# S5 discretisation on VectorE, projection tiles behind every scan batch, and four merge gates kept in HBM

## The chip, the cores and the metric

The kernel runs on one core of a Trainium2 chip, as one program, launched once. The metric is device time in microseconds. A core has five engines that run on their own and wait for each other by semaphores: TensorE (PE, matrix products into PSUM), VectorE (DVE), ScalarE (ACT), GpSimd (POOL) and SyncE (SP). DMAs are issued from queues of SP, ACT and POOL. Everything here is in float32, or in float32 pairs: a value is split into a rounded part `hi` and a rest `lo`, and a product is three matmuls (hi x hi, lo x hi, hi x lo).

## The reference

One step of a diffusion backbone of two layers on 512 latent tokens and 128 context tokens (T = 640 columns, D = 1024). Each layer computes, with two conditioning vectors (one per kind of token):

```python
shift, scale, gate = split(silu(cond) @ w_mod + b_mod)
h = rms_norm(x) * (1 + scale) + shift
u_a, g_a, u_b, g_b, u_c, g_c, m = split(h @ w_in)
y_a = GLU(gelu(S5_bidirectional(u_a))) * silu(g_a)     # 32 groups, 64 complex states each
y_b = Hyena2(short_conv(u_b)) * silu(g_b)              # two implicit long convolutions
y_c = pooling(u_c) * silu(g_c)
x = x + gate * (sum over b of sigmoid(m_b) * (y_b @ w_br_b)) @ w_out
```

The S5 recurrence is x[t] = a x[t-1] + B u[t] with complex a per state. Its coefficients come from the parameters by a discretisation: `dt = exp(log_dt)`, `a = exp(lam * dt)`, `k = (a - 1) / lam`, `B = k * b`. Beside the outputs y for both kinds of tokens the final S5 states of the context are returned.

## The kernel before, in words

**Projection tiles.** `h` lies in SBUF as `hhi` and `hlo`, eight blocks of 128 features by 640 tokens. `w_in` has 56 tiles of 128 output features. `win` (which calls `linear`) makes one tile: two weight chunks of 128x512 are loaded by SP (`wr`, three buffers), ACT casts each to `wh` (L238), DVE makes the rest `wl` (L239), and PE runs 4 x 3 matmuls of 320 columns for each chunk and each half of the tokens (L261 to L263), 48 in all. A callback evicts each half from PSUM, for which there are three buffers.

**Stages.** The *head* loads x, squares it, makes the modulation vectors (`mod_chunk`, L404, 2 MB of weights each, and `mod_turn`, L415), the filter network (`mlp`), the S5 discretisation for both layers (`s5_disc`, `exp_`, `s5_disc2`, `s5_bb`) and `h` (`make_h`), and puts the Hyena filters of layer 0 into HBM (`filter`). Then each layer runs:
- `layer`: `u_a` (four projection tiles, through HBM into another order), then eight scan batches (`s5_gen` makes matrices and rotations for four groups, with `kd` stored to HBM by SP and scattered back by eight DMAs into `mt`, L914; `s5_run` makes the inputs `pz`, the scans `kk` on DVE, L961 and L962, the output `yp`, L974 and L976, and the GELU, stored to `yd`). After the eight batches, in the program's text, twelve `conv_u` tiles (short convolution, evicted into `raw`, L996) and four `gate_b` tiles (SiLU into `sgb`, L1012; POOL multiplies).
- `glu` (four SiLU gates `sga`, then the GLU), the Hyena convolutions, the pooling branch, and the first merges.
- `merges`: for branch a one tile at a time (`merge`), for b and c two tiles at a time (`merge2`, eight calls per layer). `merge2` takes the two gate tiles of the projection from `win2` (L333 to L335), which forms them with seven products of 12 matmuls in place of eight by adding up blocks of weights and of `h` beforehand (`win2_prep`, on DVE), and then multiplies them onto the branch's product (`branch`, L1225, 24 matmuls for each tile). In layer 0 a modulation chunk for later use goes between the calls.
- `out_proj` and the norm.

**What sets the order.** Nothing is ordered by hand. The instructions are put into each engine's queue by a planner at compile time. The order of the program's text is its priority; it simulates the engines and takes an instruction of lower priority when those before it are not ready. Once planned, the queues are fixed: on the chip an engine waits for the next instruction of its queue, whatever else is ready, and the same holds for SP's and POOL's DMA queues.

The discretisation works on tiles of 128x64 (two directions of 64 states, and for both layers 32 groups), its powers on up to 128x256, and `s5_bb` on 128x512. It is a chain of some hundred instructions on POOL, with three activations on ACT (two sines and an absolute value, L746 to L748) and a reciprocal on DVE.

Of the kernel before, what the change touches and what calls it, by code (L numbers as in the profile page):

```python
# [14 lines left out]
ALU = mybir.AluOpType  # L15
# [207 lines left out]
class Body:  # L223
    def __init__(self, nc, tc, I, O, dbg=None):
        self.nc, self.tc, self.I, self.O, self.dbg = nc, tc, I, O, dbg or {}
        self.smod, self.sacc = {}, {}
# [473 lines left out]
    def exp_(self, pool, x):  # L700
        nc = self.nc
        v = nc.gpsimd
# [11 lines left out]
        v.tensor_scalar(o, c, 1.0 / 40320, 1.0 / 5040, op0=ALU.mult, op1=ALU.add)  # L714
        for f in (720, 120, 24, 6, 2, 1, 1):
            v.tensor_tensor(out=o, in0=o, in1=c, op=ALU.mult)
            v.tensor_scalar(o, o, 1.0 / f, None, op0=ALU.add)
        v.tensor_scalar(q, q, 127.0, 8388608.0, op0=ALU.add, op1=ALU.mult)
        v.tensor_copy(qi, q)
        v.tensor_tensor(out=o, in0=o, in1=qi.bitcast(F32), op=ALU.mult)  # L720
        return o

    def s5_disc(self, Q, S):
        nc, I = self.nc, self.I
        v = nc.gpsimd
        w = DEPTH * G
        sp = Q.tile([P, 5, DEPTH, G], F32, name="sp")
        for l in range(DEPTH):
            nc.sync.dma_start(sp[:, :, l], I['s5p'][l])
# [61 lines left out]
    def s5_bb(self, Q, S, l, kre, kim):  # L791
# [5 lines left out]
        self.cmul(nc.gpsimd, Q, self.bb[:, 0], self.bb[:, 1], kb(kre), kb(kim), sm[:, 0], sm[:, 1], [G, H], "cb")  # L797

    def s5_disc2(self, Q, S, pw, rs):
        nc = self.nc  # L800
        nc.gpsimd.dma_start(self.pwd, pw[:, :, :, 1])
        nc.gpsimd.dma_start(self.rsd, rs[:, :, 1])
# [204 lines left out]

    def silu_tile(self, l, nt, dst):
        nc = self.nc

# [197 lines left out]
    def merge2(self, l, n, br, ys):  # L1208
        ths = [self.M.tile([P, 644], F32, tag="t", name="mth", bufs=4)[:, 0:T] for _ in range(2)]
        self.win2(l, 32 + 8 * br + n, ths)  # L1210
# [64 lines left out]
    def run(self):  # L1275
        tc, nc = self.tc, self.nc
        with tc.tile_pool(name="dram", bufs=1, space=DRAM) as self.DR, \
# [10 lines left out]
            self.setup()  # L1288
# [7 lines left out]
            with self.pool("mod0") as M, self.pool("filt0") as F:  # L1296
                with self.pool("disc", side="left") as Q, self.pool("mlp", side="left") as FM:
                    fh = self.mlp(FM, fh)
                    wins = F.tile([P, 5, 512], F32, name="wins")
                    fr = F.tile([P, 3, 2, 3 * P], F32R, name="fr")  # L1300
                    self.setup_par()
                    self.mod_open(0, M)
                    self.load_x0(X, 0)
                    for kk in range(KD):
                        self.square(X, kk, 0)
# [10 lines left out]
                    self.s5_disc2(Q, SP, *dd)  # L1316
# [170 lines left out]
```

## Time and profile before

| | |
|---|---|
| median of 3 runs (lowest to highest) | 1569.88 us (1569.44 to 1576.25) |
| the profiled execution: own time, span | 1571.28 us, 1569.3 us |
| mean granted TensorE clock of it | 0.957 of full speed |
| PE busy | 1447.5 us, 92% of the span, 10764 matmuls |
| DVE busy | 1144.9 us, 73% |
| ACT busy | 683.2 us, 44% |
| POOL busy | 624.7 us, 40% |
| DMA | 173.49 MB, mean 111 GB/s |

The profile is of one execution. Busy times are sums of what the engine's instructions cover; issuing a DMA and waiting are not counted. The granted clock is the share of TensorE's full speed that the chip allowed; its two levels are 1.2 and 2.4 GHz. A bracket behind a row of a timeline says how long the engine stood before it and what it waited for. The shares over the whole span hide that the stages have different limits, so the rows below go by stages.

### The profile page before, as it was taken

Reading aid. Unit: us, or ns where it says so; the run is one execution under the profiler, and the core shown is the slowest. Engines: PE = TensorE matmul, PEld = TensorE weight load, DVE = VectorE, ACT = ScalarE, POOL = GpSimd, SP = SyncE. Lnnn points to the kernel's source line nnn. Section 1 sums busy time; section 2 is a strip of 40 time slices with the busy share of each in tenths; the row PEclk is TensorE's granted clock in tenths of the full one; section 3 lists DMA queues with packets and bytes.
Section 4 is the critical chain, followed back from the end, with each engine's and each line's share of the span. In section 5 each row is a group of like instructions: output and inputs, shape, how many; then the busy total and the mean of one; then the engine's idle time right before and its main releaser. Section 6 shows DMA issues by size and latency. Waiting matters only on the chain.

```text
span 1569.3 us, 28424 instructions
## 1 busy us (share of the span) xinstructions
PE 1447.5 (92%) x10764; PEld 1381.5 (88%) x10764; DVE 1144.9 (73%) x1896; ACT 683.2 (44%) x1474; POOL 624.7 (40%) x608
## 2 busy tenths in 40 slices
PE   4769898899999999999998788879999999999997
PEld 2458897899999998999997788879999999999996
DVE  6688899945777795555577888996377779766665
ACT  3166454525333443444334655453443334444443
POOL 5917254320344325454323635542015243566411
PEclk8789989999999999999999988989999999999998
DMA  9424312243222334554652342122532213222154
GB/s 311 158 72 118 98 53 70 69 122 107 91 75 81 102 121 135 184 172 137 190 181 100 104 114 60 52 69 84 146 96 83 74 61 121 82 83 85 36 168 155
DMA packets 114944, 173.49 MB, mean 111 GB/s; under 512 B 30360, under 2 KB 54568, under 8 KB 114297
## 3 DMA queue, kind: packets, MB, share of 16 engines
q1 hardware_dynamic: 113433, 165.33, 34.4%
q0 software_dynamic: 1296, 6.19, 1.2%
q8 instruction: 85, 1.39, 0.4%
q14 instruction: 50, 0.41, 0.1%
q10 hardware_dynamic: 80, 0.16, 0.0%
HBM read 150.08 MB, written 21.56 MB: 109 GB/s over the span
## 4 chain that ended last, share of the span: by engine, by line
PE 64%; DVE 16%; issue 6%; DMA 5%; POOL 3%; ACT 3%; SPq 2%; POOLq 0%; DVEq 0%; ACTq 0%
PE mm L261 13%; PE mm L262 13%; PE mm L263 13%; PE mm L333 4%; PE mm L335 4%; PE mm L334 4%; DVE wl L239 2%; PE modp L404 2%; PE inva L1131 1%; PE invb L1131 1%; DVE kk L962 1%; DVE kk L961 1%; DVE i L874 1%; DMA wr<-w_in 1%; DMA yr<-yd 1%
## 5 line engine op out<-in xcount | busy, mean ns | idle before, releaser
L261 PE MATMUL mm<-hhi,wh 128*128 128x320 f32 x1280 | 404.9, 317 | 21.9 <-ACT raw L996 12.3
L263 PE MATMUL mm<-hhi,wl 128*128 128x320 f32 x1280 | 400.1, 315 | 7.4 <-DVE wl L239 7.4
L262 PE MATMUL mm<-hlo,wh 128*128 128x320 f32 x1280 | 403.3, 315 | 2.5 <-DVE hlo L665 1.8
L239 DVE TENSOR_TENSOR wl<-wr,wh 128x512 fp32r<-128x512 f32 x312 | 258.8, 831 | 106.2 <-ACT wh L238 98.6
L238 ACT CAST wh<-wr 128x512 fp32r<-128x512 f32 x312 | 192.7, 618 | 247.2 <-PE mm L262 172.1
L261 PEld LDWEIGHTS mm<-hhi,wh 128*128 128x128 f32 x1280 | 246.2, 192 | 27.0 <-ACT raw L996 13.7
L263 PEld LDWEIGHTS mm<-hhi,wl 128*128 128x128 f32 x1280 | 245.3, 192 | 8.2 <-DVE wl L239 7.9
L262 PEld LDWEIGHTS mm<-hlo,wh 128*128 128x128 f32 x1280 | 246.1, 192 | 4.6 <-DVE hlo L665 2.2
L875 POOL TENSOR_TENSOR i<-i,i 128x1024 f32<-128x1024 f32 x16 | 45.2, 2822 | 136.7 <-DVE i L873 104.1
L262 PE MATMUL mm<-mlo,wh 128*128 128x320 f32 x256 | 79.6, 312 | 0.5 <-DVE mlo L242 0.4
L261 PE MATMUL mm<-mhi,wh 128*128 128x320 f32 x256 | 79.0, 312 | 0.9 <-DVE X L1249 0.6
L333 PE MATMUL mm<-hhi,wh 128*128 128x320 f32 x256 | 79.8, 312 | 0.0
L335 PE MATMUL mm<-hhi,wl 128*128 128x320 f32 x256 | 79.4, 310 | 0.0
L263 PE MATMUL mm<-mhi,wl 128*128 128x320 f32 x256 | 78.8, 309 | 0.4 <-DVE wl L239 0.4
L334 PE MATMUL mm<-hlo,wh 128*128 128x320 f32 x256 | 79.0, 309 | 0.0
L239 DVE TENSOR_TENSOR wl<-ws,wh 128x512 fp32r<-128x512 f32 x64 | 54.4, 849 | 31.4 <-ACT wh L238 30.1
L1225 DVE SCALAR_TENSOR_TENSOR mth<-mth,mm 128x320 f32<-128x320 f32 x64 | 31.2, 488 | 54.8 <-PE mm L263 54.8
L238 ACT CAST wh<-ws 128x512 fp32r<-128x512 f32 x64 | 39.7, 620 | 71.9 <-PE mm L334 36.3
L339 DVE TENSOR_TENSOR mth<-mm,mth 128x320 f32<-128x320 f32 x80 | 39.2, 491 | 34.7 <-PE mm L335 18.1
L335 PE MATMUL mm<-thi,wl 128*128 128x320 f32 x192 | 60.6, 316 | 0.0
L333 PE MATMUL mm<-thi,wh 128*128 128x320 f32 x192 | 60.5, 315 | 0.0
L873 POOL TENSOR_TENSOR ow<-cw,po 128x512 f32<-128x512 f32 x32 | 45.9, 1451 | 34.7 <-PE yp L976 34.6
(424 smaller groups left out, 3988.5 us busy)
## 6 DMA issues: line engine op xcount, KB each, us to landing
wr<-w_in SPq DMA_DIRECT2D x224, 256.0 KB
wm<-w_mod SPq DMA_DIRECT2D x48, 512.0 KB
wr<-w_out SPq DMA_DIRECT2D x48, 256.0 KB
hd<-hs SPq DMA_DIRECT2D x32, 256.0 KB
hsr<-hd SPq DMA_DIRECT2D x32, 256.0 KB
mt<-kd SPq DMA_DIRECT2D x128, 32.0 KB
wr<-w_br_a SPq DMA_DIRECT2D x16, 256.0 KB
wr<-w_br_b SPq DMA_DIRECT2D x16, 256.0 KB
```

The costliest lines, as they stand in the source:

```text
L238: nc.scalar.copy(hi, src)
L239: nc.vector.tensor_tensor(out=lo, in0=src, in1=hi.bitcast(F32), op=ALU.subtract)
L261: nc.tensor.matmul(ps[i], wh[:, ks], at(hi, k, sl), start=(k == 0), stop=False)
L262: nc.tensor.matmul(ps[i], wh[:, ks], at(lo, k, sl), start=False, stop=False)
L263: nc.tensor.matmul(ps[i], wl[:, ks], at(hi, k, sl), start=False, stop=(k == kt - 1))
L333: nc.tensor.matmul(out, wh[:, ks], xh, start=(k == 0), stop=False)
L334: nc.tensor.matmul(out, wh[:, ks], xl, start=False, stop=False)
L335: nc.tensor.matmul(out, wl[:, ks], xh, start=False, stop=(k == 3))
L339: e.tensor_tensor(out=o, in0=x, in1=y, op=ALU.add)
L404: nc.tensor.matmul(ps[r0:r0 + 32, :], self.cs[:, 2 * hf + q, :], w[:, q, :], start=(hf < 2), stop=(hf >= 2))
L873: eng.tensor_tensor(out=out[:, r], in0=hb(r), in1=pb(0), op=ALU.mult)
L875: e.tensor_tensor(out=out, in0=out, in1=tmp, op=ALU.add)
```

## The change

Five parts:
1. The discretisation (`exp_`, `s5_disc`) runs on DVE in place of POOL, with multiply and add fused into one instruction (the Horner steps of `exp_` are seven `scalar_tensor_tensor`). Its parameters `s5p` are loaded by `s5_load`, which is called before `setup`, so these are the first loads of the kernel.
2. `s5_bb` of layer 0 runs on DVE (that of layer 1 stays on POOL), and the two stores of `s5_disc2` (`pwd`, `rsd`, the values for layer 1) are issued from ACT's queue in place of POOL's.
3. In the head `s5_disc` comes before the squares, and `filter_load` and `s5_disc2` earlier among the modulation turns.
4. The twelve `conv_u` and four `gate_b` tiles, and four new ones, are called behind the scan batches, three and two in turn (3, 2, 3, 2, 3, 2, 3, 2), in place of after all eight.
5. The four new ones are the gate tiles 40 to 43 of the projection, the first four of branch b: `ahead` makes each with `win` (48 matmuls), evicts it with the tanh and stores it in HBM (`gd`, 128x640). `merge2` loads such tiles in place of calling `win2`, so two of the eight `merge2` of each layer have no `win2`. (`silu_tile` has the same test; no tile that it makes is kept.)

```diff
     def exp_(self, pool, x):
-        nc = self.nc
-        v = nc.gpsimd
+        v = self.nc.vector
...
-        v.tensor_scalar(o, c, 1.0 / 40320, 1.0 / 5040, op0=ALU.mult, op1=ALU.add)
-        for f in (720, 120, 24, 6, 2, 1, 1):
-            v.tensor_tensor(out=o, in0=o, in1=c, op=ALU.mult)
-            v.tensor_scalar(o, o, 1.0 / f, None, op0=ALU.add)
-        v.tensor_scalar(q, q, 127.0, 8388608.0, op0=ALU.add, op1=ALU.mult)
-        v.tensor_copy(qi, q)
-        v.tensor_tensor(out=o, in0=o, in1=qi.bitcast(F32), op=ALU.mult)
+        v.tensor_scalar(o, c, 1.0 / 40320, None, op0=ALU.mult)
+        for f in (5040, 720, 120, 24, 6, 2, 1):
+            v.scalar_tensor_tensor(out=o, in0=o, scalar=1.0 / f, in1=c, op0=ALU.add, op1=ALU.mult)
+        v.tensor_scalar(qi, q, 127.0, 8388608.0, op0=ALU.add, op1=ALU.mult)
+        v.scalar_tensor_tensor(out=o, in0=o, scalar=1.0, in1=qi.bitcast(F32), op0=ALU.add, op1=ALU.mult)
         return o
 
+    def s5_load(self, Q):
+        self.sp = Q.tile([P, 5, DEPTH, G], F32, name="sp")
+        for l in range(DEPTH):
+            self.nc.sync.dma_start(self.sp[:, :, l], self.I['s5p'][l])
+
     def s5_disc(self, Q, S):
-        nc, I = self.nc, self.I
-        v = nc.gpsimd
+        nc = self.nc
+        v = nc.vector
...
-        self.cmul(nc.gpsimd, Q, self.bb[:, 0], self.bb[:, 1], kb(kre), kb(kim), sm[:, 0], sm[:, 1], [G, H], "cb")
+        self.cmul(nc.gpsimd if l else nc.vector, Q, self.bb[:, 0], self.bb[:, 1], kb(kre), kb(kim), sm[:, 0], sm[:, 1], [G, H], "cb")
 
     def s5_disc2(self, Q, S, pw, rs):
         nc = self.nc
-        nc.gpsimd.dma_start(self.pwd, pw[:, :, :, 1])
-        nc.gpsimd.dma_start(self.rsd, rs[:, :, 1])
+        nc.scalar.dma_start(self.pwd, pw[:, :, :, 1])
+        nc.scalar.dma_start(self.rsd, rs[:, :, 1])
...
+    def ahead(self, l, nt, func, scale, U):
+        nc = self.nc
+        st = U.tile([P, L642 + 2], F32, tag="raw", name="gst", bufs=2)[:, 0:T]
+
+        def cb(half, ps):
+            nc.scalar.activation(st[:, half * HT:half * HT + HT], ps, func, scale=scale)
+
+        self.win(l, nt, cb)
+        self.gd[l, nt] = self.DR.tile([P, T], F32, name=f"gd{l}_{nt}")
+        nc.sync.dma_start(self.gd[l, nt], st)
...
     def merge2(self, l, n, br, ys):
         ths = [self.M.tile([P, 644], F32, tag="t", name="mth", bufs=4)[:, 0:T] for _ in range(2)]
-        self.win2(l, 32 + 8 * br + n, ths)
+        nt = 32 + 8 * br + n
+        if (l, nt) in self.gd:
+            for i in range(2):
+                self.nc.sync.dma_start(ths[i], self.gd[l, nt + i])
+        else:
+            self.win2(l, nt, ths)
...
-            self.setup()
...
                 with self.pool("disc", side="left") as Q, self.pool("mlp", side="left") as FM:
+                    self.s5_load(Q)
+                    self.setup()
                     fh = self.mlp(FM, fh)
-                    wins = F.tile([P, 5, 512], F32, name="wins")
-                    fr = F.tile([P, 3, 2, 3 * P], F32R, name="fr")
                     self.setup_par()
                     self.mod_open(0, M)
                     self.load_x0(X, 0)
+                    dd = self.s5_disc(Q, SP)
                     for kk in range(KD):
                         self.square(X, kk, 0)
...
-                    dd = self.s5_disc(Q, SP)
+                    wins = F.tile([P, 5, 512], F32, name="wins")
+                    fr = F.tile([P, 3, 2, 3 * P], F32R, name="fr")
+                    self.filter_load(0, F, wins, fr, fh)
                     self.mod_turn(0, 2, self.mod_chunk(0, 2, M, "mm"), "mm")
                     self.mod_turn(0, 3, self.mod_chunk(0, 3, M, "mm"), "mm")
-                    self.filter_load(0, F, wins, fr, fh)
+                    self.s5_disc2(Q, SP, *dd)
                     self.mod_turn(0, 0, self.mod_chunk(0, 0, M, "mm"), "mm")
                     rr = [r for r, _ in self.rinv((0, 1), nc.vector, "mm")]
                     self.mod_turn(0, 1, self.mod_chunk(0, 1, M, "mm"), "mm")
-                    self.s5_disc2(Q, SP, *dd)
...
+            beside = [lambda i=i: self.conv_u(l, i, vx[i // 4][:, i % 4, :], SP) for i in range(12)]
+            beside += [lambda i=i: self.gate_b(l, i, S, vx[2]) for i in range(4)]
+            beside += [lambda i=i: self.ahead(l, 40 + i, AF.Tanh, 0.5, SP) for i in range(4)]
             for b in range(NB):
                 g = self.s5_gen(l, b, S)
                 self.s5_run(l, b, S, g)
+                for _ in range(3 - b % 2):
+                    beside.pop(0)()
             nc.sync.dma_start(self.O['ns'][l], self.nst)
-            for i in range(12):
-                self.conv_u(l, i, vx[i // 4][:, i % 4, :], SP)
-            for i in range(4):
-                self.gate_b(l, i, S, vx[2])
```

## Rows read from the trace of the kernel before

**Rows 1.** Busy time by stage: us, busy (xcount) of each engine, clock, DMA.

```profile
core 0: us, PE busy (x) PEld busy (x) DVE busy (x) ACT busy (x) POOL busy (x), PEclk, DMA share, GB/s
0.00:62.00 62.00, 35.11 (x126) 18.17 (x128) 40.00 (x91) 18.64 (x38) 40.33 (x76) 0.81 0.82 268
62.00:84.00 22.00, 10.68 (x75) 7.99 (x74) 15.99 (x2) 2.85 (x6) 21.52 (x41) 0.68 0.35 101
...
150.00:345.00 195.00, 174.60 (x1642) 169.84 (x1631) 164.91 (x230) 90.52 (x231) 72.58 (x43) 0.93 0.28 77
...
909.00:1104.00 195.00, 174.30 (x1653) 168.34 (x1653) 164.49 (x232) 92.30 (x235) 76.13 (x44) 0.93 0.28 77
...
1341.00:1497.00 156.00, 155.55 (x1060) 154.76 (x1058) 101.50 (x153) 69.15 (x129) 88.62 (x74) 1.00 0.24 72
```

**Rows 2.** Timeline of POOL in the head, first and last of some hundred instructions.

```profile
19.21 3.00 POOL L708 TENSOR_SCALAR ex<-sp 128x64 f32<-128x64 f32 x1 [16.66 <-DMA sp<-s5p]
...
82.30 1.37 POOL L698 TENSOR_TENSOR bb<-cb,cb 128x512 f32<-128x512 f32 x1
```

**Rows 3.** Timeline of ACT in the head.

```profile
46.14 0.26 ACT L746 ACTIVATE q<-q 128x64 f32<-128x64 f32 x1 [9.33 <-POOL q L438]
...
66.62 0.35 ACT L825 COPY rsl<-rs 128x192 f32<-128x192 f32 x1 [9.06 <-POOL rs L779]
```

**Rows 4.** Timeline of DVE in the head, rows for prices by size.

```profile
86.85 0.42 DVE L239 TENSOR_TENSOR flp<-hq,fhp 128x256 fp32r<-128x256 f32 x1
...
88.14 0.16 DVE L606 TENSOR_TENSOR rt<-rt,rx 64x10 f32<-64x10 f32 x1
...
94.22 0.69 DVE L239 TENSOR_TENSOR flo<-hc,fhi 128x512 fp32r<-128x512 f32 x1 [3.02 <-ACT fhi L238]
```

**Rows 5.** Timeline of DVE in the head, around its two long instructions.

```profile
47.25 0.50 DVE L239 TENSOR_TENSOR flp<-hq,fhp 128x256 fp32r<-128x256 f32 x1 [6.24 <-ACT fhp L238]
...
68.01 7.45 DVE L239 TENSOR_TENSOR flo<-hc,fhi 128x512 fp32r<-128x512 f32 x1 [6.69 <-ACT fhi L238]
75.39 8.84 DVE L559 SCALAR_TENSOR_TENSOR hc<-hx,hc 128x512 f32<-128x512 f32 x1
84.15 0.41 DVE L521 TENSOR_TENSOR hq<-fwp,wins 128x256 f32<-128x256 f32 x1
```

**Rows 6.** Evictions on ACT by line, 100 to 420: count, min/median/max ns, first and last start.

```profile
L996 ACT COPY raw<-mm x36: 262/314/431, 155.7 to 307.1; 128x320 f32<-128x320 f32 x12, 128x192 f32<-128x192 f32 x12, 128x128 f32<-128x128 f32 x12
...
L1012 ACT ACTIVATE sgb<-mm x8: 431/436/440, 318.2 to 344.2; 128x320 f32<-128x320 f32 x8
```

**Rows 7.** Timeline of PE, 91 projection matmuls in a row.

```profile
150.71 0.31 PE L261 MATMUL mm<-hhi,wh 128*128 128x320 f32 x1
...
163.91 0.31 PE L261 MATMUL mm<-hhi,wh 128*128 128x320 f32 x1
```

**Rows 8.** PE's groups, 150 to 345: busy us, mean ns | idle before, releaser.

```profile
L261 PE MATMUL mm<-hhi,wh 128*128 128x320 f32 x260 | 83.3, 320 | 6.3 <-ACT raw L996 6.3
...
L976 PE MATMUL yp<-w,ow 128*128 128x81 f32 x128 | 21.4, 294 | 1.3 <-DVE w L968 1.3
L974 PE MATMUL yp<-ug,mt 128*128 128x81 f32 x64 | 13.3, 292 | 9.0 <-DMA wr<-w_in 6.2 <-DMA mt<-kd 2.8
...
L884 PE MATMUL trp<-cst,i 128*128 128x128 f32 x56 | 9.7, 327 | 3.5 <-ACT it L885 3.5
```

**Rows 9.** Chain of waits in layer 0's merges: start, us; two chunks one call apart.

```profile
648.72 1.85 PE modp L404 x16
...
671.03 1.85 PE modp L404 x16
```

**Rows 10.** Busy time of two more stretches, columns as in rows 1.

```profile
583.00:627.00 44.00, 44.00 (x283) 38.29 (x285) 25.19 (x42) 17.13 (x33) 22.98 (x19) 1.00 0.51 166
0.00:40.00 40.00, 18.24 (x50) 9.73 (x50) 26.02 (x68) 14.28 (x28) 20.33 (x39) 0.86 0.95 313
```

**Rows 11.** Timelines of SP's queue and of PE around 285 us.

```profile
282.39 3.60 SPq L914 DMA_DIRECT2D mt<-kd  x8
...
288.43 0.69 PE L974 MATMUL yp<-ug,mt 128*128 128x81 f32 x2 [4.25 <-DMA wr<-w_in]
```

More of the change, by code (lines that the diff above doesn't have):

```diff
@@ L225, in __init__ @@
         self.nc, self.tc, self.I, self.O, self.dbg = nc, tc, I, O, dbg or {}
-        self.smod, self.sacc = {}, {}
+        self.smod, self.sacc, self.gd = {}, {}, {}
     def dump(self, name, ap):
@@ L713, in exp_ @@
         self.madd(v, c, q, hi - math.log(2.0), c, o)
-        v.tensor_scalar(o, c, 1.0 / 40320, 1.0 / 5040, op0=ALU.mult, op1=ALU.add)
-        for f in (720, 120, 24, 6, 2, 1, 1):
-            v.tensor_tensor(out=o, in0=o, in1=c, op=ALU.mult)
-            v.tensor_scalar(o, o, 1.0 / f, None, op0=ALU.add)
-        v.tensor_scalar(q, q, 127.0, 8388608.0, op0=ALU.add, op1=ALU.mult)
-        v.tensor_copy(qi, q)
-        v.tensor_tensor(out=o, in0=o, in1=qi.bitcast(F32), op=ALU.mult)
-        return o
+        v.tensor_scalar(o, c, 1.0 / 40320, None, op0=ALU.mult)
[3 more added lines that the diff above has]
+        v.scalar_tensor_tensor(out=o, in0=o, scalar=1.0, in1=qi.bitcast(F32), op0=ALU.add, op1=ALU.mult)
+        return o
+    def s5_load(self, Q):
+        self.sp = Q.tile([P, 5, DEPTH, G], F32, name="sp")
+        for l in range(DEPTH):
+            self.nc.sync.dma_start(self.sp[:, :, l], self.I['s5p'][l])
     def s5_disc(self, Q, S):
-        nc, I = self.nc, self.I
-        v = nc.gpsimd
+        nc = self.nc
+        v = nc.vector
         w = DEPTH * G
-        sp = Q.tile([P, 5, DEPTH, G], F32, name="sp")
-        for l in range(DEPTH):
-            nc.sync.dma_start(sp[:, :, l], I['s5p'][l])
+        sp = self.sp
         lr, li, ld = sp[:, 0], sp[:, 1], sp[:, 2]
@@ L1006, in conv_u @@
                                        op0=ALU.mult, op1=ALU.add)
+    def ahead(self, l, nt, func, scale, U):
[6 more added lines that the diff above has]
+        nc.sync.dma_start(self.gd[l, nt], st)
     def silu_tile(self, l, nt, dst):
         nc = self.nc
+        if (l, nt) in self.gd:
+            nc.sync.dma_start(dst[:, 0:T], self.gd[l, nt])
+            return
         def cb(half, ps):
@@ L1209, in merge2 @@
         ths = [self.M.tile([P, 644], F32, tag="t", name="mth", bufs=4)[:, 0:T] for _ in range(2)]
-        self.win2(l, 32 + 8 * br + n, ths)
+        nt = 32 + 8 * br + n
+        if (l, nt) in self.gd:
+            for i in range(2):
+                self.nc.sync.dma_start(ths[i], self.gd[l, nt + i])
+        else:
+            self.win2(l, nt, ths)
         for i in range(2):
```

## The prediction

> **What bounds the kernel now.** I read the table of busy time by stage first [rows 1]. TensorE (PE) is the engine that the end hangs on: from the merges of layer 1 on (1341 to 1497 us) it is busy 155.55 of 156 us at a granted clock of 1.00, so whatever PE work is taken out there is taken off the time. Three stretches are different. In the head PE is busy 35.1 of the first 62 us and 10.7 of the next 22, and in the two scan stages (150 to 345 and 909 to 1104, 195 us each) it is busy 174.6 and 174.3 us at a mean clock of 0.93. Those are the places with something to win, and the change works on all three.
>
> **Head.** GpSimd (POOL) carries the S5 discretisation. The timeline of POOL shows it begin at 19.21, when the parameters have landed after an idle 16.66 us, and run almost without a gap to 82.30 + 1.37 = 83.7 us [rows 2]. Three things are seen to wait for it. ScalarE (ACT) stands 9.33 us before the first sine and 9.06 us before the copy of `rsl` [rows 3], and what is queued behind these on ACT makes VectorE (DVE) stand 6.24 and 6.69 us. Then two DVE instructions of 128x512, which cost 0.69 elsewhere [rows 4], take 7.45 and 8.84 us, one after the other, and the second ends when POOL's run ends [rows 5]. That is 6.24 + 6.69 + (7.45 - 0.69) + (8.84 - 0.69) = 27.8 us of DVE. Behind it sit the evictions that PE needs to go on (PE has 10.68 busy us in the 22 from 62 to 84 [rows 1]) and the normalisation of x, which releases the first projection.
>
> What of this goes, and what comes: `exp_` falls from 25 instructions to 15 (its multiply and add pairs are fused) and stands there twice. With range reduction, coefficients and powers DVE gets 81 instructions: 68 of 128x64, one copy and six products of 128x128, six of 128x256; `s5_bb` adds six of 128x512. By the rows of 64x10 at 0.16, 128x256 at 0.42 and 128x512 at 0.69 [rows 4], a straight line gives some 0.2 for 64 and 0.28 for 128 elements: 68 x 0.2 + 7 x 0.28 + 6 x 0.42 + 6 x 0.69 = 13.6 + 2.0 + 2.5 + 4.1 = 22 us. DVE has 62 - 40 = 22 idle us before 62 us [rows 1]; 6.2 of them are the wait just counted, so 16 can take new work, and with its loads first in SyncE's (SP) queue the discretisation can start well before 19 us. I take half of that, 8 us, as used, because the chain is dependent and goes through ACT for the sines. Then 14 us of the 22 lie on DVE's path, and the head ends 27.8 - 14 = **14 us** earlier; bounds 6 (nothing hidden) and 22 (all 16 hidden). The two stores of `pwd` and `rsd` go from POOL's queue to ACT's, at about a microsecond of issue, beside work; nothing. The two loads of `s5p`, now ahead of `cst` and of the loads of the filter network, put these off by about a microsecond, in a time when DVE waits for data anyway; `filter_load`, now ahead of the first modulation turns, moves loads and no work that PE waits for; nothing for both.
>
> Here a rule speaks against the gain. The rows show two DVE instructions held through a row of POOL instructions, which last up to 1.4 us each, for 14.9 us together [rows 2, 5]. The Trainium skill, "SBUF — State Buffer", section "Who interferes with whom", says that a VectorE instruction with two SBUF inputs and a GpSimd instruction that reads SBUF exclude each other, and that the later one waits until the first *instruction* is through. By the letter of it the two waits would be one POOL instruction each, about 2 us, and most of the 14.9 would have some other cause that may stay; by the trace, all of it ends with POOL's run. I go by the trace, and price the other case below.
>
> **Scan stage, each layer.** Before, the twelve `conv_u` tiles already run inside the scan although they are written after it: their evictions run from 155.7 to 307.1, and the four `gate_b` tiles follow as a block, 318.2 to 344.2 [rows 6]. So the order is a planner's, and the new place in the program is a priority, not a command. What is new work is `ahead`: four tiles of 48 matmuls. From 150.71 to 163.91 PE issues 90 of them, 0.147 us each [rows 7]; one tile is 7.05 us, four are **28.2 us** more PE work in the stage. What can take them: PE's waits, 6.3 for evicted tiles, 1.3 and 9.0 before the output products, 3.5 before the transposes, 20 us in all [rows 8], and the clock, 7% of 174.6, 12 us at most. DVE is the engine that could refuse: busy 164.9 of 195 [rows 1]. The tiles add eight weight splits of 0.69, 5.5 us, so some 170 of it would be used; it becomes the second bound, not the first. Most of the waits come from DVE and ACT being late while the convolution tiles press on DVE, and from weights that sit behind the scatter of `mt` in SP's queue. With more filler PE should become the limit, and these engines run ahead of it. I take 12 of the 20 us and 8 of the 12 as used: the stage gets 195 + 28.2 - 12 - 8 = **203 us, 8 longer**. Bounds: nothing used, 28.2 longer; all used, 4 shorter. The four stores of 320 KB per layer are one issue each on SP; each waits for its second eviction, and behind it in SP's queue stand the next weights and the next `mt`. I take nothing, since three weight buffers cover 7 us; if that cover is gone, see the second rival. ACT gets eight evictions and eight casts, some 8 us, and has 104 idle us [rows 1].
>
> **Merges, each layer.** The first two of eight `merge2` lose their `win2`: 7 products of 12 matmuls, 84 x 0.147 = 12.3 us each. The pitch confirms the count: between two modulation chunks lie 671.03 - 648.72 = 22.31 us [rows 9], which is 132 x 0.147 + 1.85 and about a microsecond of `modt`. PE has no gap there, so **24.7 us** go per layer. The `win2_prep` work on DVE stays and has less time before the first `win2` that is left; the two removed ones give DVE about as much back. In layer 0 the modulation chunks come too: two pairs now need 2 x (0.5 + 0.65 + 2.1) = 6.5 MB (weights, kept gates, chunk) in about 20 us, 325 GB/s, against 166 now and 313 in the first 40 us, when the queues were 95% busy [rows 10]. I charge **2 us**, with bounds 0 and 10. Layer 1 has no chunks and pays nothing.
>
> **Sum.** 14 + 2 x (24.7 - 8) - 2 = 45 us off the profiled execution's own 1571.28: 1526. The median of the runs shown, 1569.88, is 1.4 below that execution, so the forecast for a median is 1571.28 - 45.4 - 1.4 = **1524 us**.
>
> **Rivals.** (1) The planner does not do what the program order says, or DVE holds PE back as before, and the 28.2 us lengthen the stage in full: each layer loses 28.2 - 24.7 = 3.5, and only the head gains: 1571.3 - 14 + 7 + 2 - 1.4 = 1565. For it: DVE is busy in 85% of the stage, and more than that while convolution tiles run, since the `gate_b` tiles at its end ask little of it. Against: 30 us of DVE are idle [rows 1], five times what the new splits need. Chance 0.11. (2) **Slower: SP's queue.** In every batch SP issues eight scatters of `mt`, 3.60 us, once `kd` is back from HBM, and the weights stand behind them; at 288.43 PE waited 4.25 us for weights in this way [rows 11]. With five weight loads per batch in place of three, and a store among them, such a wait could fall on each batch: 8 x 4.25 x 2 = 68 us, 1592. It decides from (45 + 8) / 16 = 3.3 us per batch. Against: only 6.2 us of the 9.0 in the row were waits for weights in the whole stage [rows 8]. Chance 0.07. (3) The head does not gain, because DVE, now with 22 us more, ends it as late as POOL did, or because the hold had another cause than POOL's run, which stays: 1524 + 14 = 1538. Chance 0.11. (The rule of the page named above would speak for the second.) (4) PE's waits and clock are all filled: 2 x 12 us more, 1500, and 1494 with some more of the head. Chance 0.11. My forecast has 0.6.
>
> **Numbers.** The range is 1494 to 1558: it holds the forecast, rivals 3 and 4 and the unhidden ends of single terms, and leaves out the slower rival and most of rival 1. About 0.5%, 8 us, is what a measurement of this kernel can tell from no change, so faster means below 1562. Forecast, rivals 3 and 4 and a little of rival 1 make 0.84 faster; the rest of rival 1 makes 0.09 the same; 0.07 slower.
>
> **What would show it.** Right: no DVE instruction of some 8 us before 90 us, and the first projection's evictions some 14 us earlier; `sgb` and the new evictions inside the scan, a stage near 203 us with a clock above 0.93 and fewer PE waits; two merge iterations of about 10 us of PE in each layer with no wait for `mth` or `wm`. Wrong: `ahead` tiles in a block after the last scan; PE waits for `wr<-w_in` in most batches; DVE without a gap to the old end of the head; PE waiting for `wm` in layer 0's merges.

## The result and the profile after

The changed kernel takes **1534.03 us** (median of 4 runs, 1530.10 to 1534.17) against 1572.48 (1569.44 to 1576.25) for the kernel before, run beside it: a ratio of 0.9748 with an interval of 0.9718 to 0.9779, 38 us faster. The forecast was 1524, the range 1494 to 1558; it was set from the 1569.88 known then, and as a gain it is 45.4 us, of which 38.4 came. The profiled execution took 1534.17 us, its span is 1532.4, against 1569.3 before.

First the page of the changed kernel, its parts 1 and 2 (40 slices of 38.3 us):

```profile
span 1532.4 us, 28365 instructions
...
PE 1435.3 (94%) x10812; PEld 1372.2 (90%) x10812; DVE 1125.5 (73%) x1951; ACT 672.0 (44%) x1454; POOL 524.9 (34%) x473
...
PE   3998899999999999999998897989999999999997
...
PEclk9899999999999999999998899999999999999998
```

PE's lower digits are left in the head, in the first part of both scan stages and at the turn between the layers. Now the stretches of [rows 1], moved to where these stages lie now: head (two), scan stage of layer 0, two windows of layer 0's merges with the modulation chunks (against [rows 10]), scan stage of layer 1, merges of layer 1.

```profile
core 0: us, PE busy (x) PEld busy (x) DVE busy (x) ACT busy (x) POOL busy (x), PEclk, DMA share, GB/s
0.00:62.00 62.00, 34.17 (x168) 17.93 (x169) 52.81 (x176) 27.07 (x57) 1.47 (x6) 0.90 0.91 299
62.00:84.00 22.00, 21.22 (x131) 17.18 (x131) 20.91 (x51) 11.93 (x24) 2.39 (x2) 0.89 0.19 73
130.00:343.00 213.00, 196.35 (x1795) 191.04 (x1794) 172.32 (x237) 98.23 (x249) 74.07 (x49) 0.96 0.32 89
560.00:600.00 40.00, 40.00 (x257) 34.01 (x256) 28.23 (x59) 12.54 (x26) 9.51 (x9) 1.00 0.62 204
600.00:640.00 40.00, 40.00 (x276) 37.33 (x275) 20.23 (x34) 16.23 (x31) 18.76 (x16) 1.00 0.54 178
878.00:1092.00 214.00, 196.42 (x1856) 191.45 (x1854) 174.70 (x241) 100.67 (x255) 77.29 (x51) 0.97 0.32 90
1340.00:1460.00 120.00, 119.58 (x815) 118.98 (x813) 75.91 (x113) 53.44 (x99) 67.88 (x57) 1.00 0.23 67
```

Where the time went is read from the starts of a few landmark instructions. The evictions of the changed kernel by line on ACT: `u_a` (L678, the end of the head), `gst` (L1013, the kept gates, now the last thing in the scan stage) and `sgb`, `sga` (both L1026).

```profile
L678 ACT COPY ua<-mm x12: 427/498/752, 88.5 to 129.6; 128x320 f32<-128x320 f32 x4, 128x192 f32<-128x192 f32 x4, 128x128 f32<-128x128 f32 x4
...
L1026 ACT ACTIVATE sgb<-mm x8: 427/432/439, 268.9 to 305.4; 128x320 f32<-128x320 f32 x8
...
L1013 ACT ACTIVATE gst<-mm x8: 431/436/439, 311.6 to 342.4; 128x320 f32<-128x320 f32 x8
...
L1026 ACT ACTIVATE sga<-mm x8: 415/435/476, 350.5 to 371.1; 128x320 f32<-128x320 f32 x8
```

And the `win2` matmuls (L335) of layer 0 and of layer 1, whose last ones mark the end of the merges' gates; before there were 96 of each, here 72:

```profile
L335 PE MATMUL mm<-thi,wl x72: 308/309/394, 602.8 to 725.2; 128*128 128x320 f32 x72
...
L335 PE MATMUL mm<-thi,wl x72: 308/309/312, 1343.0 to 1449.7; 128*128 128x320 f32 x72
```

The ledger, in us, each line from one landmark to the next (before from the same lines of its profile):

| part | before | after | change | forecast |
|---|---|---|---|---|
| head, to the last `u_a` eviction | 149.0 | 129.6 | -19.4 | -14 |
| scan stage, layer 0, to the last `sgb` or `gst` | 195.2 | 212.8 | +17.6 | +8 |
| gate block `sga` | 30.1 | 28.7 | -1.4 | 0 |
| to the last `win2` of layer 0 | 378.5 | 354.1 | -24.4 | -24.7 + 2 |
| to layer 1's last `u_a` | 155.1 | 153.2 | -1.9 | 0 |
| scan stage, layer 1 | 195.4 | 212.3 | +16.9 | +8 |
| `sga` | 29.2 | 29.7 | +0.5 | 0 |
| to the last `win2` of layer 1 | 354.0 | 329.3 | -24.7 | -24.7 |
| to the end | 82.8 | 82.7 | -0.1 | 0 |

The sum is -36.9. Two terms are well off: the head gave 5 us more, and each scan stage took 9 us more than forecast. Per layer the change was worth 8.2 and 7.3 us, where 14.7 and 16.7 were forecast.

The line between the head and layer 0's scan stage is drawn by an eviction, and in the changed kernel that eviction comes late on ACT. PE itself starts the first scan batch at these times, before and after:

```profile
148.18 1.03 PE L884 MATMUL trp<-cst,i 128*128 128x128 f32 x8
...
125.64 1.03 PE L884 MATMUL trp<-cst,i 128*128 128x128 f32 x8
```

By this landmark the head gave 22.5 us, and layer 0's stage took 20.7 more; in layer 1 (910.96 and 881.10) the stage took 17.3 more.

**Scan stage.** PE's groups in it, 130 to 343 (beside [rows 8]):

```profile
L261 PE MATMUL mm<-hhi,wh 128*128 128x320 f32 x318 | 101.9, 321 | 5.1 <-ACT raw L996 5.1
...
L976 PE MATMUL yp<-w,ow 128*128 128x81 f32 x128 | 20.3, 283 | 0.3 <-DVE w L968 0.2
L974 PE MATMUL yp<-ug,mt 128*128 128x81 f32 x64 | 13.6, 296 | 8.0 <-DMA mt<-kd 8.0
...
L944 PE MATMUL pz<-ug,it 128*64 128x82 f32 x128 | 11.6, 248 | 3.3 <-DMA ug<-ud 3.3
```

There are 16.7 us of waits left of 20.4. The waits for `wr` (6.2) and `it` (3.5) went, but that for `mt` rose from 2.8 to 8.0, and that for `ug` from 0.3 to 3.3. In layer 1 the wait for `mt` was there before the change too (window 909 to 1104), and it grew a little (878.6 to 1091.5):

```profile
L974 PE MATMUL yp<-ug,mt 128*128 128x81 f32 x64 | 14.3, 310 | 9.4 <-DMA mt<-kd 9.1 <-issue 0.2
...
L974 PE MATMUL yp<-ug,mt 128*128 128x81 f32 x64 | 12.7, 280 | 11.5 <-DMA mt<-kd 11.5
```

So before `yp` PE waits for SP's transfers about as long as it did: 9.0 and 8.0 us in layer 0, under two names, 9.1 and 11.5 in layer 1. In e1 below, without the kept gates, it is 7.2 us for `mt` in layer 0 and nothing for weights. What the filler took are the waits for evictions, `it` and `w`: 11.1 us before and 5.3 after in layer 0, 11.1 and 4.4 in layer 1. The SP queue around the longest wait for `mt`, and PE behind it (beside [rows 11]):

```profile
249.78 0.33 SPq L252 DMA_DIRECT2D wr<-w_in  x1
251.16 0.33 SPq L910 DMA_DIRECT2D kd<-kh  x1
252.98 3.61 SPq L914 DMA_DIRECT2D mt<-kd  x8
```

```profile
258.21 0.69 PE L974 MATMUL yp<-ug,mt 128*128 128x81 f32 x2 [3.63 <-DMA mt<-kd]
```

**Head.** The discretisation on DVE starts at 8.46, and its sine is on ACT at 24.3, where [rows 3] had it at 46.14; the normalisation `ht` begins at 71.2 against 98.1 before. DVE has no instruction of 7 or 8 us any more: the long ones of [rows 5], L239 and L559, cost 0.68 and 0.67. From DVE's timeline, then the two lines' own views:

```profile
8.46 0.20 DVE L707 TENSOR_SCALAR ex<-sp 128x64 f32<-128x64 f32 x1 [5.30 <-DMA sp<-s5p]
...
53.22 0.68 DVE L239 TENSOR_TENSOR flo<-hc,fhi 128x512 fp32r<-128x512 f32 x1
...
54.42 0.69 DVE L698 TENSOR_TENSOR bb<-cb,cb 128x512 f32<-128x512 f32 x1
55.36 0.67 DVE L559 SCALAR_TENSOR_TENSOR hc<-hx,hc 128x512 f32<-128x512 f32 x1
```

```profile
L746 ACT ACTIVATE q<-q x1: 240/240/240, 24.3 to 24.3; 128x64 f32<-128x64 f32 x1
...
L661 DVE SCALAR_TENSOR_TENSOR ht<-X,sg,rr x18: 344/536/1194, 71.2 to 100.7; 128x320 f32<-128x320 f32 x6, 128x192 f32<-128x192 f32 x6, 128x128 f32<-128x128 f32 x6
```

**Merges of layer 0**, for which 2 us were charged: in the two windows from 560 to 640 the queues carry 204 and 178 GB/s, more than the 166 of [rows 10], and PE has no gap. Nothing was paid.

### The profile page after: what moved, and what is told of

Same layout as the page of the kernel before. It is cut to its first block, busy times and chain, and to the rows that moved or that the text cites. A ratio compares the mean times of both kernels' runs of the same rounds, so it can differ in the third digit from the quotient of the medians.

```text
span 1532.4 us, 28365 instructions
## 1 busy us (share of the span) xinstructions
PE 1435.3 (94%) x10812; PEld 1372.2 (90%) x10812; DVE 1125.5 (73%) x1951; ACT 672.0 (44%) x1454; POOL 524.9 (34%) x473
## 4 chain that ended last, share of the span: by engine, by line
PE 68%; DVE 15%; DMA 6%; issue 5%; ACT 3%; SPq 2%; POOL 1%; POOLq 0%; ACTq 0%; DVEq 0%
PE mm L261 15%; PE mm L263 15%; PE mm L262 15%; PE mm L333 3%; PE mm L335 3%; PE mm L334 3%; DVE wl L239 2%; PE inva L1145 1%; SPq L914 1%; DVE i L874 1%; PE invb L1145 1%; PE yp L976 1%; PE modp L404 1%; DVE vx L1003 1%; DVE hlo L665 1%
## 5 line engine op out<-in xcount | busy, mean ns | idle before, releaser
L261 PE MATMUL mm<-hhi,wh 128*128 128x320 f32 x1408 | 446.1, 318 | 15.3 <-ACT raw L996 9.0
L263 PE MATMUL mm<-hhi,wl 128*128 128x320 f32 x1408 | 440.4, 314 | 8.5 <-DVE wl L239 6.3
L262 PE MATMUL mm<-hlo,wh 128*128 128x320 f32 x1408 | 442.4, 314 | 0.5 <-DVE hlo L659 0.4
L239 DVE TENSOR_TENSOR wl<-wr,wh 128x512 fp32r<-128x512 f32 x316 | 265.9, 843 | 114.4 <-ACT wh L238 111.5
L261 PEld LDWEIGHTS mm<-hhi,wh 128*128 128x128 f32 x1408 | 269.9, 192 | 20.8 <-ACT raw L996 10.0
L263 PEld LDWEIGHTS mm<-hhi,wl 128*128 128x128 f32 x1408 | 269.5, 192 | 9.5 <-DVE wl L239 6.8
L262 PEld LDWEIGHTS mm<-hlo,wh 128*128 128x128 f32 x1408 | 270.1, 192 | 1.7 <-DVE hlo L659 1.2
L1246 POOL TENSOR_TENSOR macc<-macc,mth 128x320 f32<-128x320 f32 x32 | 35.0, 1099 | 86.4 <-DVE mth L1244 86.4
L239 DVE TENSOR_TENSOR wl<-ws,wh 128x512 fp32r<-128x512 f32 x48 | 42.7, 889 | 29.7 <-ACT wh L238 28.6
L333 PE MATMUL mm<-hhi,wh 128*128 128x320 f32 x192 | 59.9, 312 | 0.0
L335 PE MATMUL mm<-hhi,wl 128*128 128x320 f32 x192 | 59.4, 309 | 0.0
L334 PE MATMUL mm<-hlo,wh 128*128 128x320 f32 x192 | 59.4, 309 | 0.0
L1052 POOL TENSOR_TENSOR ps<-pu 128x663 f32<-128x663 f32 x8 | 12.3, 1540 | 120.4 <-ACT pu L1045 120.4
L1246 POOL TENSOR_TENSOR acc<-acc,mth 128x320 f32<-128x320 f32 x32 | 37.7, 1179 | 44.4 <-DVE mth L1244 44.3
```

The source lines that it names most:

```text
L239: nc.vector.tensor_tensor(out=lo, in0=src, in1=hi.bitcast(F32), op=ALU.subtract)
L261: nc.tensor.matmul(ps[i], wh[:, ks], at(hi, k, sl), start=(k == 0), stop=False)
L262: nc.tensor.matmul(ps[i], wh[:, ks], at(lo, k, sl), start=False, stop=False)
L263: nc.tensor.matmul(ps[i], wl[:, ks], at(hi, k, sl), start=False, stop=(k == kt - 1))
L333: nc.tensor.matmul(out, wh[:, ks], xh, start=(k == 0), stop=False)
L334: nc.tensor.matmul(out, wh[:, ks], xl, start=False, stop=False)
```

## The experiments

Twelve kernels in three groups (e1 to e4, e5 to e8, e9 to e12); kernels of a group ran on one chip with the kernel before among them, and ratios are against that: its medians were 1568.72, 1567.63 and 1572.91. The changed kernel itself ran beside the third group only, so a difference to it from the first two is given by medians and by ratios.

### What each part is worth: e1, e2, e3, e4

**e1_head_only**: the changed kernel with the scan stage of before (and so no kept gates).

```diff
-            beside = ...
-                for _ in range(3 - b % 2):
-                    beside.pop(0)()
             nc.sync.dma_start(self.O['ns'][l], self.nst)
+            for i in range(12):
+                self.conv_u(l, i, vx[i // 4][:, i % 4, :], SP)
+            for i in range(4):
+                self.gate_b(l, i, S, vx[2])
```

> The changed head (parts 1 to 3) with the scan stage and merges of before. Theory (the head's gain is its own: last u_a eviction at 149.0 before, 129.6 in the changed kernel): some 19 us faster than before, about 1553 us, ratio 0.988, and a last u_a eviction near 130. Rival (part of the head's gain came from what follows it): less than 10 us faster, ratio above 0.994.

Measured: 1548.07 us (1545.12 to 1549.38), ratio 0.9861 [0.9836, 0.9886]: 20.7 below the 1568.72 beside it. The last `u_a` starts at 128.9, the stage to the last `sgb` is 193.7. So the head alone is worth some 20 us, more than half of the whole, and it leaves the scan stage almost as it was. Its new order of calls (part 3 of the change) was not run by itself.

**e2_no_kept**: the sixteen old tiles behind the batches, two each, and no kept gates.

```diff
-            beside += [lambda i=i: self.ahead(l, 40 + i, AF.Tanh, 0.5, SP) for i in range(4)]
...
-                for _ in range(3 - b % 2):
+                for _ in range(2):
```

> The changed head, the twelve convolution tiles and four gate_b tiles two behind each batch, no gate kept, all eight win2 in the merges. Theory A (the planner filled the scan with tiles before too, so the place in the program alone does nothing): as the head alone, about 1553 us, scan stage 195 us. Theory B (the tight place behind the batch itself fills PE's waits): the stage falls by about 10 us per layer, 1533 us, and the kept gates then give nothing of their own.

Measured: 1543.35 (1541.64 to 1548.90), ratio 0.984 [0.9811, 0.9869]. It is 4.7 below e1, with intervals that overlap, and half way between the two expected times. In its profile the stage is 190.1 and 187.6 us in the two layers, against 193.7 and 192.9 in e1. The place of the old tiles is thus worth some 5 us; the planner had moved most of them already [rows 6].

From e2 to the changed kernel the spans fall by 8.1 us (1540.5 to 1532.4), the medians by 9.3, by the ratios it is 0.9% or 14. That is what the kept gates bring. By the landmarks the stage grows by 22.7 and 24.7 us, the merges give back 24.4 and 24.7, the `sga` block is 3.5 and 1.3 shorter, and the head of this execution 1.4. So in these two profiles the stage takes nearly all that the merges save, and most of the gain lies in the `sga` block. In the profile of e11, the changed kernel beside the third group, the stages are 209.4 and 210.5 us, so the growth over e2 is 19.3 and 22.9, and the `sga` blocks are 3.6 and 2.4 shorter.

**e3_block**: all twenty tiles, kept gates too, written after the last batch.

```diff
+            for i in range(4):
+                self.ahead(l, 40 + i, AF.Tanh, 0.5, SP)
```

> The changed head and the four kept gates, but all twenty tiles written after the eight batches, as before. Theory A (only work placed behind the batches fills the scan): the kept tiles stand as a block of 28 us after the scan and give back the 24.7 saved in the merges; about 1553 + 7 = 1560 us. Rival (the planner fills the scan with lower priority work wherever it is written): as the changed kernel, about 1534 us.

Measured: 1552.50 (1551.32 to 1553.52), ratio 0.9893 [0.9866, 0.992]: 4.4 slower than e1. Its ACT evictions of the kept gates:

```profile
L1013 ACT ACTIVATE gst<-mm x8: 431/438/476, 330.4 to 355.2; 128x320 f32<-128x320 f32 x8
```

They follow `sgb` (to 325.5) as a block of nearly 30 us, and the stage is 224.0, 30.3 longer than e1's. For the kept gates the place in the program does decide: as a block they cost 4 us more than they save, between the batches they save some 8 more than they cost.

**e4_loads_first**: the kernel before, with the loads of `s5p` first; the discretisation stays on POOL.

```diff
+    def s5_load(self, Q):
+        self.sp = Q.tile([P, 5, DEPTH, G], F32, name="sp")
...
-            self.setup()
...
+                    self.s5_load(Q)
+                    self.setup()
```

> The kernel before with one edit: the two loads of s5p first; the discretisation stays on POOL. Theory (POOL's run sets the head and starts some 10 us earlier): about 9 to 11 us faster than before, ratio 0.993, with the two long DVE instructions still there, some 10 us earlier. Rival (the engine is what matters, DVE's long instructions only move): within 3 us of before.

Measured: 1568.81 (10 runs, 1566.06 to 1574.88), ratio 0.9994 [0.9974, 1.0013]: nothing. POOL's run now begins at 8.42 and ends at 64, 20 us earlier, and yet the last `u_a` is at 146.8 instead of 149.0. In DVE's timeline of e4, and POOL's beside it:

```profile
55.36 0.41 DVE L557 SCALAR_TENSOR_TENSOR hc<-hx 128x256 f32<-128x256 f32 x1
55.80 8.46 DVE L523 TENSOR_TENSOR hq<-hq,br 1x256 f32<-1x256 f32 x1
64.30 0.69 DVE L555 TENSOR_TENSOR hc<-hx 128x512 f32<-128x512 f32 x1
```

```profile
55.92 0.72 POOL L697 TENSOR_TENSOR pw<-pc,pc 128x256 f32<-128x256 f32 x1
...
61.39 1.37 POOL L697 TENSOR_TENSOR bb<-cb,cb 128x512 f32<-128x512 f32 x1
62.61 1.36 POOL L698 TENSOR_TENSOR bb<-cb,cb 128x512 f32<-128x512 f32 x1
```

One DVE instruction is again held until POOL's run ends, another one this time (L523, 0.42 in the changed kernel). `ht` starts at 91.7 (98.1 before, 71.2 after). So an earlier POOL run moves the hold, and the head hardly gains; the loads alone are not what the head's 20 us come from. A second difference was not held fixed: from 50 to 70 us TensorE's granted clock is 0.50 of full speed in e4 (56 matmuls, after 7 in the 10 us before), against 0.93 in the kernel before (102 matmuls). What e4's head would be at the same clock is not known.

### What POOL does to DVE: e5

**e5_pool_beside**: the changed kernel, with 28 products on POOL in the head that nobody reads.

```diff
+        for i in range(28):
+            nc.gpsimd.tensor_tensor(out=jk[:, i % 2], in0=pj[:, 0, 0:256], in1=pj[:, 1, 0:256], op=ALU.mult)
```

> The changed kernel with 28 products of 128x256 added on POOL behind the discretisation (about 20 us from 45 us on); nothing reads their result, so no engine waits for them but POOL itself. Theory (POOL's run of instructions holds DVE by itself, as the trace of before showed): one or more DVE instructions of several us stand beside the run, together 8 to 15 us of hold, and the last u_a eviction comes 6 to 12 us later than in the changed kernel, about 1543 us. Rival (a DVE instruction waits for one POOL instruction at most, 0.7 us): no DVE instruction above 2 us there, a head within 2 us of the changed kernel's, about 1534 us.

Measured: 1542.81 (1538.19 to 1546.22), ratio 0.9834 [0.9799, 0.9868]: above the changed kernel by 9 us in the medians and by 13 in the ratios. The last `u_a` is at 144.5 instead of 129.6 (the profile is of the execution of 1546.22). The time is the one expected. The POOL run, and three of DVE's instructions in it (in the changed kernel the first two take 0.68 and 0.69, the third 0.42):

```profile
47.05 28.99 POOL L806 TENSOR_TENSOR jk<-pw 128x256 f32<-128x256 f32 x28 [44.55 <-DVE pw L698]
```

```profile
53.48 1.21 DVE L694 TENSOR_TENSOR cb<-rs,s5b 128x512 f32<-128x512 f32 x1
54.62 1.21 DVE L696 TENSOR_TENSOR cb<-rs,s5b 128x512 f32<-128x512 f32 x1
55.75 0.94 DVE L697 TENSOR_TENSOR pw<-pc,pc 128x256 f32<-128x256 f32 x1
```

Both engines slow each other: a POOL product takes 28.99 / 28 = 1.04 instead of 0.72 (L697 in e4), a DVE product of 128x512 takes 1.21 instead of 0.69, one of 128x256 0.94 instead of 0.42. The same 29 us of e5, and then of the changed kernel:

```profile
47.00:76.00 29.00, 26.60 (x140) 19.33 (x138) 28.76 (x40) 13.45 (x29) 28.95 (x28) 0.74 0.53 161
```

```profile
47.00:76.00 29.00, 27.90 (x174) 19.77 (x167) 25.32 (x61) 17.89 (x37) 0.86 (x1) 0.83 0.45 139
```

DVE got 40 instructions done instead of 61, PE 140 matmuls instead of 174. DVE's L520, which reads one of its two inputs (`fw`, from PE) in PSUM, takes 1.21 beside POOL's run and 1.22 without it. This is a cost of POOL's work on DVE, shown with DVE's own work unchanged. It is not the whole loss: `ht` starts 10.3 us later than in the changed kernel, the last `u_a` 14.9. From 80 to 90 us the granted clock is 0.53 (after 28 matmuls in the 10 us before), where the changed kernel has 1.00 at that point of its head (70 to 80). No DVE instruction of the stretch from 47 to 76 us lasts over 1.22 us, so the sign that was expected with the time did not come. The rule cited in the prediction (the Trainium skill, "SBUF — State Buffer", section "Who interferes with whom": the later one waits for one instruction of the other) fits e5, half a microsecond per instruction; it doesn't fit the 7.45 and 8.84 of [rows 5] nor the 8.46 of e4. What makes one DVE instruction wait through a whole row of POOL's there stays open. It is not always to the end of the row: the 7.45 of [rows 5] ended at 75.46, while POOL's run went on to 83.67. And it goes both ways: in the kernel before, while DVE's instructions follow one another from 57 to 61 us, a POOL instruction of 128x64, 0.37 elsewhere, lasts as long as this:

```profile
57.68 3.15 POOL L717 TENSOR_SCALAR exo<-exo 128x64 f32<-128x64 f32 x1
```

With the work off POOL neither form is left in this stretch.

### What limits the scan stage: e6, e7, e8

**e6_mixed**: tiles with heavy and light work for DVE mixed evenly over the batches, in place of all convolutions first.

```diff
+            beside = [cv(8), ah(0), cv(9), cv(10), gb(0), cv(11), ah(1), cv(0), gb(1), cv(1),
+                      cv(2), ah(2), cv(3), gb(2), cv(4), cv(5), ah(3), cv(6), gb(3), cv(7)]
```

> The changed kernel with its twenty tiles in another order: convolution tiles (heavy on DVE) mixed evenly with the light ones (gate_b and kept gates), so that each batch has one or two of each. Theory A (the stage is lost in its first half, where DVE is full with convolution tiles, while DVE has room in the second): the stage falls from 213 to about 203 us per layer, about 1515 us. Rival B (PE waits for the scatter of mt and for buffers, whatever stands beside): the stage stays at 213 us within 3, about 1534 us.

Measured: 1538.48 (1535.77 to 1540.78), ratio 0.9808 [0.978, 0.9836]: no gain; a loss of 4 us by medians, 9 by ratios. The stage, here to the last eviction of `raw`, is 214.5 us. PE's three longest waits in it:

```profile
PE yp L976 <- DVE w L968: 5.8, 4, 1.7
PE yp L974 <- DMA mt<-kd: 4.4, 2, 3.4
PE pz L944 <- DMA ug<-ud: 2.6, 1, 2.6
```

The waits change their names (`w` from 0.2 to 5.8, `mt` from 8.0 to 4.4), and all together they are 15.7 us against 16.7. Spreading DVE's load over the stage in this way does not shorten it.

**e7_mt_act**: the eight scatters of `mt` per batch issued from ACT's queue instead of SP's, to take away the wait that was the largest.

```diff
-            nc.sync.dma_start(mt[t_ * H:t_ * H + H], kv[0:H, :, (7 - t_) * H:(7 - t_) * H + P])
+            nc.scalar.dma_start(mt[t_ * H:t_ * H + H], kv[0:H, :, (7 - t_) * H:(7 - t_) * H + P])
```

> The changed kernel with the eight scatters of mt per batch issued from ACT's queue in place of SP's. Theory B (weights and mt block each other in SP's queue; PE waited 8.0 and 11.5 us for mt): these waits go, 6 to 10 us per layer, about 1518 us. Rival (the wait is the way of kd through HBM, or ACT now holds its own casts behind kd): no gain, 1534 us or up to 20 us more.

Measured: 1553.17 (1551.24 to 1557.06), ratio 0.9908 [0.9879, 0.9938], slower than the changed kernel by 19 us in the medians and 25 in the ratios. PE's waits in the stage (132 to 353):

```profile
PE mm L261 <- ACT raw L996: 22.5, 5, 8.7
PE mm L263 <- DVE wl L239: 4.3, 3, 2.7
PE yp L974 <- DMA mt<-kd: 1.4, 1, 1.4
```

The wait for `mt` fell from 8.0 to 1.4 as meant, and PE's wait for the evictions rose from 5.1 to 22.5: the scatters wait for `kd`, and on ACT the evictions and casts that PE needs stand behind them. ACT itself stands 49 us in this stage until the scatters are out, 12.7 of them before an eviction (L996) and the others here:

```profile
ACT z L956 <- DMA mt<-kd: 36.3, 5, 10.4
```

On SP only transfers stand behind. Here the engine whose queue carries the waiting transfer paid, and PE with it. In layer 1 the wait for evictions rose less, from 3.9 to 9.6.

**e8_eight**: eight kept gates per layer, three tiles behind each batch, so four of eight `merge2` without `win2`.

```diff
-            beside += [lambda i=i: self.ahead(l, 40 + i, AF.Tanh, 0.5, SP) for i in range(4)]
+            beside += [lambda i=i: self.ahead(l, 40 + i, AF.Tanh, 0.5, SP) for i in range(8)]
...
-                for _ in range(3 - b % 2):
+                for _ in range(3):
```

> The changed kernel with eight kept gates per layer, three tiles behind every batch (24), and four win2 left. Theory (the changed stage has 17 us of PE waits and some slow clock left per layer, of which about a third can be filled): the stage grows by 20 to 26 us and the merges lose 24.7, so within 5 us of the changed kernel per layer; 1525 to 1537 us. Rival (the fill goes on as for the first four, 11 of 28 us covered): the stage grows by 17 us, about 1519 us.

Measured: 1526.95 (1522.37 to 1528.77), ratio 0.973 [0.9698, 0.9762]. The stage of e8:

```profile
131.00:367.00 236.00, 226.16 (x2016) 221.07 (x2015) 173.70 (x249) 110.11 (x272) 72.50 (x49) 0.98 0.35 103
```

It is 235.0 us, 22.2 longer than in the changed kernel, for another 28.2 us of PE work; the clock rises from 0.96 to 0.98, PE's idle time falls from 16.7 to 9.8, DVE's busy time hardly grows (172.3 to 173.7). In layer 1 the stage grows by 19.3. Beside e11 on one chip (e12 below) the growth is 26.2 and 21.7 us, while the merges give back 22.2 and 24.7 and the `sga` block is 3.8 and 3.5 shorter. So the stage takes in the second set, too, at 0.7 to 0.9 of its price, and the set is worth a little again; by how much, e12 tells.

### The loads, another queue, and the best version: e9 to e12

**e9_loads_late**: the changed kernel with the loads of `s5p` behind those of x.

```diff
-                    self.s5_load(Q)
                     self.setup()
...
                     self.load_x0(X, 0)
+                    self.s5_load(Q)
                     dd = self.s5_disc(Q, SP)
```

> The changed kernel with the two loads of s5p where they stood before, behind those of x. Theory (the early loads let DVE do the discretisation in its idle time while x is on its way; before, the parameters landed at 19.2 us, now at 8.5): the chain starts some 10 us later, DVE loses some 5 to 8 us of idle time that it could fill, and the last u_a eviction comes 4 to 8 us later; about 1540 us. Rival (only the engine matters, as the kernel with POOL's discretisation and early loads suggests): within 2 us of the changed kernel, 1534 us.

Measured: 1538.65, but spread from 1532.25 to 1548.65, ratio 0.9789 [0.9744, 0.9835]; the changed kernel beside it took 1530.65. In its profile, of the execution of 1548.65, `ht` starts at 93.5 instead of 71.2 and the last `u_a` at 143.8:

```profile
L678 ACT COPY ua<-mm x12: 430/499/748, 108.7 to 143.8; 128x320 f32<-128x320 f32 x4, 128x192 f32<-128x192 f32 x4, 128x128 f32<-128x128 f32 x4
```

In that execution most of the head's gain is gone; in another the time is that of the changed kernel. What the load order is worth beside the change is not settled: 8 us by the medians, 2 to 18 by single runs.

**e10_gpq**: e8 with the scatters of `mt` on POOL's queue (`nc.gpsimd.dma_start` in the line of e7).

> Eight kept gates per layer, and the scatters of mt issued from POOL's queue in place of SP's. Theory (the scatter holds whatever queue it stands in while kd is on its way; POOL's products of the next batch stand behind it, as ACT's casts did): slower than with SP, 1535 to 1560 us. Rival (POOL has 160 idle us in the stage and can take the hold): PE's waits for mt and weights go, up to 4 us per layer faster, about 1520 us.

Measured: 1527.05 (1523.06 to 1532.56), ratio 0.9709 [0.9674, 0.9743]. PE waits no more for `mt`, a wait for `ug` of 4.7 is the longest, and the time is 5 us above that of e8's kernel beside it (e12, below; the intervals overlap). POOL's queue does no such harm as ACT's, and brings nothing either. But with eight kept gates there was little left to bring: in e12, with SP's queue, PE waits for `mt` 0 and 0.9 us in the two stages.

**e11_changed_again** and **e12_eight_again**: the changed kernel and e8's, unchanged, on one chip.

> The changed kernel once more, on the chip of the runs beside it: 1534 us, ratio 0.975 to the kernel before.

> Eight kept gates per layer once more, beside the changed kernel on one chip. Theory (the stage grows by 22 us, the merges lose 24.7): 5 us under the changed kernel, 1527 to 1530 us. Rival (no difference beyond the spread): within 2 us of it.

Measured: 1530.65 (6 runs, 1529.84 to 1533.35), ratio 0.9735 [0.9707, 0.9763], and 1522.26 (6 runs, 1520.05 to 1523.99), ratio 0.9679 [0.9651, 0.9707]. The runs of the two do not overlap: eight kept gates beat four by 8.4 us. **e12 is the best version found**, 50 us below the kernel before.

## Why the prediction was right, and where it was not

The direction, the range and the places were right. The result is 10 us above the forecast: 2.6 of them are the base (1572.48 beside it, in place of 1569.88), and the rest is two mis-sized terms with opposite signs. That the head gave more than forecast is luck, as far as the forecast goes: without it the time would have been about 1539, by the ledger.

- **Head, 14 forecast, 19.4 measured (20.7 in e1, 22.5 by PE's start).** The step that was off is "I take half of that, 8 us, as used": if the 27.8 us all went, 8.4 of the new work lay on DVE's path by the ledger, not 14. DVE's idle time before 62 us fell from 22.0 to 9.2; the loads at the front let the work start at 8.46, in the wait for data. The instruction prices held: 0.22 for 128x64, 0.28 for 128x128, 0.42 and 0.69. The forecast has no term for TensorE's clock in the head; it rose from 0.81 to 0.90 in the first 62 us and from 0.68 to 0.89 in the next 22, and what that gave is not separated.
- **The hold on DVE** went with POOL's run, as argued from [rows 5]; rival 3 is out. The reason given was only part of it: e4 shows that with POOL's run 20 us earlier one hold of 8.46 remains and nothing is gained, and e5 shows the cost of POOL's work in another form. In both TensorE's clock was lower for a part of the head as well.
- **Scan stage, 8 longer forecast, 17.6 and 16.9 measured.** The steps that failed are "I take 12 of the 20 us" of waits and "8 of the 12" of the clock. From PE's own start of the batches (148.1 to 345 before, 125.6 to 343 after) PE's waits fell from 20.4 to 16.7, so 3.7 were taken. Its busy time rose from 176.5 to 200.7, by 24.3 in place of 28.2, so the clock, 0.93 before and 0.96 after, gave some 3.9. The two together are 7.6 of the 20 taken. The sentence "with more filler PE should become the limit, and these engines run ahead of it" came true in part for DVE and ACT, whose waits fell from 11.1 to 5.3 and 4.4, and failed for the transfers on SP, for which PE waits before `yp` as before. DVE was busy 172.3 us (about 170 forecast), and spreading its load brought nothing (e6). What sets the waits that are left is not shown.
- **Rival 1** (no fill, 28.2 longer) did not happen between the batches, but it is what e3 does: 30.3 longer when the kept gates are a block. The planner takes the program's order as a priority here. The forecast for the old tiles, that little would move, was right: 5 us (e2 against e1). But against e2, with the old tiles in their new place, the kept gates lengthen the stage by 19 to 25 us, nearer to this rival's 28.2 than to the forecast's 8.
- **Rival 2** (SP's queue, from 3.3 us per batch) had the right place and not the size: PE waits for `mt` 8.0 us in layer 0 in four waits, 11.5 in layer 1, about 1.2 us per batch, and in layer 1 it was 9.1 before. The waits for weights, that rival 2 named, are gone. A wait of 4.25 us in every batch never came.
- **Rival 4** (all filled) did not happen with four kept gates; e8's stage, with twice the filler, still idles 9.8 us.
- **Merges, -24.7 per layer**: -24.4 and -24.7 measured. The DMA charge of 2 us was not paid: PE 40.00 of 40 us at 204 GB/s.

What stays open: why single DVE instructions are held for 7 to 9 us in two kernels and in e5 never; how much the order of the loads (e9) and the new order of calls in the head are worth; how much of the head's time is TensorE's clock; what limits the scan stage. Only two queues other than SP's were tried for `mt`.

## What to carry to other kernels

Work that is moved beside a stage that is nearly full is worth what it saves at its old place less what the stage grows, and that growth is nearer to its full price than to nothing: four tiles of 28.2 us grew it by 19 to 25 here, even at 20 us of idle time and a clock of 0.93. Whether it pays depends on its place (as a block it lost 4 us, between the batches it won 8), so write it between, and try the next four too. A transfer that waits goes onto a queue with nothing behind it that the bound engine needs. A side engine's "free" run is checked against the durations of the instructions that run beside it.

## What the hardware showed that was not expected

POOL and DVE each lengthen the other when both run products from SBUF: 0.72 to 1.04 for POOL's 128x256, 0.69 to 1.21 and 0.42 to 0.94 for DVE's 128x512 and 128x256 (e5). A DVE product with one input in PSUM kept its 1.21 (L520, e5). In other mixes a single DVE instruction lasts 8.84 or 8.46 us until POOL's run ends ([rows 5], e4), even one of 1x256, or 7.45 through a part of the run; and a POOL instruction of 0.37 lasts 3.15 beside DVE's. And a POOL run that starts 11 us and ends 20 us earlier gained nothing (e4), with TensorE's clock at 0.50 in 20 us of the head.
